# Rotating the first loads over both buffer pools and keeping the last macro tile whole, in a 90-degree rotation of an 8192 x 8192 matrix

## The chip, the cores and the metric

The kernel runs on one core of one Trainium2 chip. The metric is the device time of one execution in microseconds. Times of two kernels are compared within one session on one chip, in interleaved rounds. A ratio is the mean time of one kernel's fast runs over the mean time of the other's fast runs of the same rounds, so it is not quite the ratio of the medians quoted beside it.

The profile names the engines PE (TensorE), DVE (VectorE), ACT (ScalarE) and SP (SyncE, which issues the loads here). PSUM is where PE leaves its results. A "bubble" or "hole" is a stretch in which transfers nearly stop. The "fill" is the work between the landing of the last load and the issue of the last tile's first store. The "drain" is the very end, when most DMA engines have finished.

"Loss" in this document is a stretch of time not used by the DMA: length x (1 - rate / 428 GB/s), where 428 GB/s is the rate of the long middle of the kernel. All 537.55 MB at that rate take 1256 us, so span = 1256 + sum of losses. The rates shown are rounded, so a loss over the long middle can't be read from its rate; it is taken as what is left of the span. The DMA share of a stage can come out slightly over 1.

## The reference

```python
def setup_inputs():
    return {"x": np.random.randn(8192, 8192).astype(np.float32), "k": 1}

def reference(x, k):
    return np.rot90(x, k)
```

Every output element is one input element moved. 268 MB are read and 268 MB are written.

## The kernel before

A macro tile is 1024 rows by 4096 columns, 16 tiles in all. Its rows come in eight loads of 128 rows (2 MB each). DVE reverses the columns of each load into 64 small tiles `ar` (pool of 68); PE transposes them into PSUM; ACT copies PSUM to an output buffer `ot` and issues its store (2 MB). One output needs a chunk from each of the eight loads, so no output of a tile can start before its eighth load has landed.

```python
R = 1024; RT = R // P; W = 4096; CH = 512; G = 4; PW = 2   # P = 128

def macro_tiles(N, M):
    for r0 in range(0, N, R):
        widths = [W] * (M // W)
        if r0 == 0:
            widths[:1] = [4096]
        if r0 + R == N:
            widths[-1:] = [2048, 1024, 1024]      # the last tile in three parts
        ...
# --- cut ---
    a_pool = ctx.enter_context(tc.tile_pool(name="a_pool", bufs=2))
    r_pool = ctx.enter_context(tc.tile_pool(name="r_pool", bufs=68))
    o_pool = ctx.enter_context(tc.tile_pool(name="o_pool", bufs=2))
    # PSUM pool: 2 buffers of [P, PW, R] f32
# --- cut: for each macro tile ---
        for t0 in range(0, RT, q):                # a load brings q = W // C row blocks
            if loads < 2:
                a = o_pool.tile([P, W], dt, tag="o")
            else:
                a = a_pool.tile([P, W], dt, tag="a")
            loads += 1
            nc.sync.dma_start(out=a, in_=x[...])
            # DVE: eight reversing copies a -> ar
        for g0 in range(0, C // P, G):
            ot = o_pool.tile([P, W], dt, tag="o")
            S = PW if last and g0 + G == C // P else G
            for h in range(0, G, PW):
                # PE: for w in range(PW): for t in range(RT): transpose
                nc.scalar.copy(o[:, G - PW - h : G - h, :], ps[:])
                done = h + PW
                if done % S == 0:
                    nc.scalar.dma_start(out=dst, in_=o[...])
```

## Time and profile before

| | before |
|---|---|
| median, before the prediction | 1275.13 us (1272.76 to 1278.19, 3 runs) |
| span of the profiled run | 1274.2 us |
| busy: PE, ACT, DVE | 56%, 37%, 28% |
| DMA share of the span, 100 to 1130 us | 1.01, at 428 GB/s |

From the page of the kernel before: the DMA rate in 40 equal slices of 31.9 us each, and the chain that ended last, by engine.

```profile
GB/s 375 366 427 427 427 428 431 429 428 428 430 428 430 428 427 429 429 429 429 427 427 427 429 427 428 427 427 429 428 427 426 424 423 429 427 425 422 420 408 338
...
DMA 84%; DVE 12%; issue 2%; ACT 1%; PE 0%; DVEq 0%; SPq 0%; ACTq 0%
```

The middle is flat at 428: the DMA is the bound, and only the first two slices and the last few are below it. The table of stages of the kernel before shows the same (the columns are the stretch, its length, busy time and instructions of each engine, the granted PE clock, the DMA share, and GB/s):

```profile
20.00:60.00 40.00, 14.01 (x84) 11.74 (x85) 17.29 (x50) 7.37 (x4) 0.00 (x0) 1.00 0.94 364
...
100.00:1130.00 1030.00, 603.11 (x3360) 578.19 (x3360) 291.37 (x840) 381.39 (x210) 0.00 (x0) 0.74 1.01 428
1130.00:1200.00 70.00, 42.08 (x278) 40.01 (x279) 16.65 (x48) 32.73 (x18) 0.00 (x0) 0.83 1.01 424
1200.00:1248.00 48.00, 26.23 (x172) 24.72 (x170) 9.52 (x28) 19.85 (x11) 0.00 (x0) 0.79 1.00 406
1248.00:1272.00 24.00, 12.85 (x96) 12.06 (x96) 1.58 (x5) 12.87 (x8) 0.00 (x0) 0.79 0.85 354
1272.00:1274.20 2.20, 0.00 (x0) 0.00 (x0) 0.00 (x0) 0.00 (x0) 0.00 (x0) 0.50 0.06 22
```

The stretch 20 to 60 us loses 6.0 us, and all from 1130 us on loses 9.4 us. The Trainium skill ("DMA: Bandwidth & Descriptors", Specifications) gives 435 GB/s as the ceiling of the fabric; the 428 of this trace's middle is within 2% of that, so by that figure the middle has under 2% to give, and the change doesn't touch it.

In the timeline of DVE (start, length, instruction, idle time before it and what ended it) each row of eight copies follows the landing of a load:

```profile
22.76 2.77 DVE L111 COPY ar<-a 128x512 f32<-128x512 f32 x8 [2.12 <-DMA a<-in_x_dram]
29.79 2.77 DVE L111 COPY ar<-a 128x512 f32<-128x512 f32 x8 [4.25 <-DMA a<-in_x_dram]
35.39 2.77 DVE L111 COPY ar<-a 128x512 f32<-128x512 f32 x8 [2.83 <-DMA a<-in_x_dram]
42.46 2.77 DVE L111 COPY ar<-a 128x512 f32<-128x512 f32 x8 [4.29 <-DMA a<-in_x_dram]
47.89 2.77 DVE L111 COPY ar<-a 128x512 f32<-128x512 f32 x8 [2.66 <-DMA a<-in_x_dram]
```

The first of these rows is load 4 of the first tile and the last row is load 8. They are 7.0, 5.6, 7.1 and 5.4 us apart, where a 2.097 MB load takes 4.9 us at 429 GB/s. Only two load buffers turn over there.

In the last 20 us, the timeline of ACT of the kernel before shows copies 5.5 us apart, with waits for stores:

```profile
1251.91 3.63 ACT L133 COPY ot<-ps 128x2048 f32<-128x2048 f32 x2 [1.95 <-PE ps L128]
1255.58 0.55 ACTq L141 DMA_DIRECT2D out_dram<-ot  x1
1257.39 3.64 ACT L133 COPY ot<-ps 128x2048 f32<-128x2048 f32 x2 [1.85 <-DMA out_dram<-ot]
```

### The profile page before, as it was taken

To read this page: it belongs to the slowest core of one execution; us is meant where nothing else is said; L and a number is where in the kernel's file an instruction comes from. 1 tells how busy PE (TensorE), PEld (TensorE's weight loads), DVE (VectorE), ACT (ScalarE), POOL (GpSimd) and SP (SyncE) were. 2 spreads that over 40 slices of the span, in tenths; PEclk is the share of its full clock that TensorE was granted. 3 is DMA by queue.
4 is the path that set the end of the run, shared out by engine and by line. 5 is a ranking of instruction groups with operands and counts; after the bars stand their busy time and mean duration, and the time that the engine had idled before them with its cause. 6 is when DMAs were issued, how large, how long until landed. Compare 5 with 4: busy or idle time off the path is not lost.

```text
span 1274.2 us, 10388 instructions
## 1 busy us (share of the span) xinstructions
PE 719.2 (56%) x4096; PEld 685.5 (54%) x4096; DVE 355.2 (28%) x1024; ACT 466.9 (37%) x257; POOL 0.7 (0%) x6
## 2 busy tenths in 40 slices
PE   1455556556655665556546565565565665665564
PEld 0355556555554655556546555565555554665564
DVE  4422232223222322232223222322232222321210
ACT  0233343334334333343334333433343333434444
POOL 0000000000000000000000000000000000000000
PEclk9968686877777677776886867768777778678878
DMA  9999999999999999999999999999999999999998
GB/s 375 366 427 427 427 428 431 429 428 428 430 428 430 428 427 429 429 429 429 427 427 427 429 427 428 427 427 429 428 427 426 424 423 429 427 425 422 420 408 338
DMA packets 39105, 537.55 MB, mean 422 GB/s; under 512 B 4112, under 2 KB 4112, under 8 KB 6160
## 3 DMA queue, kind: packets, MB, share of 16 engines
q1 hardware_dynamic: 20480, 268.44, 49.8%
q10 hardware_dynamic: 18576, 268.44, 49.8%
q8 instruction: 32, 0.52, 0.2%
q14 instruction: 17, 0.14, 0.0%
HBM read 268.44 MB, written 268.44 MB: 421 GB/s over the span
## 4 chain that ended last, share of the span: by engine, by line
DMA 84%; DVE 12%; issue 2%; ACT 1%; PE 0%; DVEq 0%; SPq 0%; ACTq 0%
DMA a<-in_x_dram 81%; DVE ar L111 12%; DMA out_dram<-ot 3%; ACT ot L133 1%; PE ps L128 0%; DVEq L111 0%; SPq L100 0%; ACTq L133 0%; ACTq L141 0%
## 5 line engine op out<-in xcount | busy, mean ns | idle before, releaser
L128 PE MATMUL ps<-ident,ar 128*128 128x128 f32 x4096 | 719.2, 358 | 543.8 <-ACT ot L133 500.2
L128 PEld LDWEIGHTS ps<-ident,ar 128*128 128x128 f32 x4096 | 685.5, 192 | 577.3 <-ACT ot L133 530.5
L133 ACT COPY ot<-ps 128x2048 f32<-128x2048 f32 x256 | 465.6, 1870 | 789.3 <-DMA out_dram<-ot 733.5
L111 DVE COPY ar<-a 128x512 f32<-128x512 f32 x1024 | 355.2, 421 | 894.4 <-DMA a<-in_x_dram 894.4
L133 ACT ACT_TABLE_LOAD x1 | 1.3, 1283 | 10.9 <-DVE ar L111 10.9
masks.py:199 POOL TENSOR_SCALAR_AFFINE_SELECT ident<-ident 128x128 f32<-128x128 f32 x1 | 0.3, 292 | 0.1
masks.py:197 POOL MEMSET ident<- 128x128 f32 x1 | 0.2, 204 | 0.3 <-POOLq L160 0.3
L160 POOL MEMSET const-bfloat16-1.0<- 128x1 bf16 x1 | 0.1, 102 | 0.0
L160 POOL MEMSET const-uint8-127<- 128x1 uint8 x1 | 0.1, 102 | 0.0
L160 POOL MEMSET const-float32-0.0<- 128x1 f32 x1 | 0.1, 99 | 0.2 <-issue 0.2
L160 POOL MEMSET const-float32-1.0<- 128x1 f32 x1 | 0.1, 99 | 0.0
## 6 DMA issues: line engine op xcount, KB each, us to landing
a<-in_x_dram SPq DMA_DIRECT2D x128, 2048.0 KB, 16.6
out_dram<-ot ACTq DMA_DIRECT2D x127, 2048.0 KB, 15.9
out_dram<-ot ACTq DMA_DIRECT2D x2, 1024.0 KB, 5.7
```

The source lines that it names most:

```text
L111: nc.vector.tensor_copy(out=ar[:], in_=a[:, u, j * CH : (j + 1) * CH].rearrange("r (b m) -> r b m", m=P)[:, :, ::-1],)
L128: nc.tensor.transpose(ps[:, PW - 1 - w, t * P : (t + 1) * P], chunks[t, g * P // CH][:, g % (CH // P), :], ident,)
L133: nc.scalar.copy(o[:, G - PW - h : G - h, :], ps[:])
L160: nc = _bacc.Bacc("TRN2", target_bir_lowering=False, num_devices=1)
```

## The change

At the start, only two of the first eight loads used the output buffers; now loads 3, 4, 7 and 8 do, so all four buffers turn over. At the end, the last macro tile is no longer cut into 2048, 1024 and 1024 columns, and its eight outputs use load and output buffers in turn, since no load needs the load buffers any more.

```diff
+LAST = [4096]
@@ macro_tiles
-        if r0 == 0:
-            widths[:1] = [4096]
         if r0 + R == N:
-            widths[-1:] = [2048, 1024, 1024]
+            widths[-1:] = LAST
@@ loads
-            if loads < 2:
+            if loads < RT and loads % 4 >= 2:
                 a = o_pool.tile([P, W], dt, tag="o")
@@ outputs
-            ot = o_pool.tile([P, W], dt, tag="o")
+            if last and g0 // G % 2 == 0:
+                ot = a_pool.tile([P, W], dt, tag="a")
+            else:
+                ot = o_pool.tile([P, W], dt, tag="o")
```

## The prediction

> **What bounds the kernel.** The DMA engines. In the stretch from 100 to 1130 us the table by stages shows a DMA share of 1.01 and 428 GB/s, and the chain of waits is 84% DMA. PE is busy 56%, ACT 37%, DVE 28%. The Trainium skill ("DMA: Bandwidth & Descriptors", Specifications) gives 435 GB/s as the fabric ceiling; this trace's middle agrees, within 2%. All 537.55 MB at 428 GB/s would take 1256 us of a 1274.2 us span. So about 18 us can be won at all, a part of it unavoidable (first packet, last completion), and only the two ends of the kernel matter.
>
> **Start, before.** The first four loads land 4.9 us apart (DVE starts at 8.1, 13.0, 17.9, 22.8: 2.097 MB each, 429 GB/s). Then only two load buffers turn over: the next four land 7.0, 5.6, 7.1 and 5.4 us apart, and the table by stages shows 351 to 375 GB/s from 20 to 45 us and 282 from 45 to 50. The change has loads 4 to 7 wait for loads 0 to 3, so about three stay in flight. I expect all eight 4.9 us apart: DVE on the eighth at 42.4 us instead of 47.9, first store issued near 48.9 instead of 54.4. That is 5.5 us; the 282 to 416 GB/s dip around 45 to 60 us should shrink too, for 0 to 1.5 us more. Estimate: 6 us, all on the critical path, since everything after is DMA-bound.
>
> **End, before.** Rate by stages: 424 (1130 to 1200), 406 (1200 to 1248), 354 (1248 to 1272), then 2.2 us of almost nothing. Against 428 that loses 0.7 + 2.5 + 4.2 us, plus the final 2 us. The last outputs start copying 5.5 us apart (1251.9, 1257.4, 1263.5), because two output buffers leave ACT waiting for stores; between 1248 and 1250 only 66 GB/s moved.
>
> **End, after.** After the last load lands, all eight outputs of the last tile (16.8 MB) remain, a pure store phase. Per output PE needs 3.7 us at full clock, ACT 3.64 + 0.55 us to issue; a store needs 4.9 to 5.0 us (the store-only stretch 1264 to 1272 averages about 422 GB/s). With four buffers the stores should queue and DMA, not ACT, set the pace. Costs: store-only rate +0.6 us; a possible bubble before the tile's first store, which is ready about 6.5 us after the last load lands, while the previous tile's last two stores cover an estimated 7.7 us: 0 to 2 us. Final latency stays, 2 us. Net gain: 7.4 - 0.6 - 1 = about 6 us. Work totals do not change.
>
> **Prediction.** 1275.1 - 12 = 1263 us, 0.9% faster; 8 in 10 between 1259 and 1270. Faster by over 2%: 0.02; within 2%: 0.97; slower by over 2%: 0.01.
>
> **What would show it.** Start: equal 4.9 us steps of the eight first loads, 425 GB/s or more from 5 to 45 us, DVE on load 8 near 42.4. Middle: unchanged 428 GB/s. End: no rate below 400 between 1130 and the last store except a short bubble; about 40 us without loads; stores landing about 5 us apart; ACT's waits for stores there, yet with DMA busy.
>
> **What would make it wrong.** PE at a lower granted clock in the dense tail (12 matmuls in 2 us at 0.57, so over 5 us per output), making the tail PE-bound: up to +8 us at the end. A store-only rate well under 420 GB/s over 40 us. A larger bubble where loads end. A read-only rate under 429 with continued loading. In the other direction, a gain of up to 15 us if all the losses vanish.

## More of the kernel before

Near 1131 us, in the steady state, a load lands 1.3 us after ACT has begun an output's copies:

```profile
1130.69 3.63 ACT L133 COPY ot<-ps 128x2048 f32<-128x2048 f32 x2 [6.25 <-DMA out_dram<-ot]
1131.95 2.78 DVE L111 COPY ar<-a 128x512 f32<-128x512 f32 x8 [7.11 <-DMA a<-in_x_dram]
```

This distance (from the start of an output's copies to DVE's start on the next landed load) is called the **offset** below.

## The result and the profile after

| | before | after |
|---|---|---|
| median, first session | 1274.65 us (1272.76 to 1278.19, 4 runs) | 1271.05 us (1270.76 to 1271.21, 4 runs) |
| ratio, first session | | 0.9968 (0.9946 to 0.9990) |
| ratio, two later sessions of 5 rounds | | 0.9952 (0.9940 to 0.9965) and 0.9950 (0.9936 to 0.9965) |

The change saves 4 us by the first session and 6 us by the two later ones. The prediction was 12 us. The measured 1271.05 lies 1 us above its range.

From the page of the kernel after, the same two lines:

```profile
GB/s 400 415 431 429 429 428 429 430 428 429 428 429 428 430 430 428 429 429 430 428 428 420 429 429 429 429 429 427 428 422 427 426 421 430 427 427 427 428 342 382
...
DMA 78%; ACT 18%; DVE 1%; PE 1%; issue 1%; ACTq 0%; DVEq 0%
```

The first slices have risen from 375 and 366 to 400 and 415. At the end the losses have moved into the last two slices: one slice has fallen to 342. Stages of the kernel after:

```profile
20.00:60.00 40.00, 14.48 (x90) 11.83 (x90) 20.10 (x59) 8.66 (x5) 0.00 (x0) 0.98 1.01 420
...
1200.00:1210.00 10.00, 5.84 (x32) 5.60 (x32) 2.96 (x10) 3.63 (x2) 0.00 (x0) 0.66 1.00 426
1210.00:1230.00 20.00, 11.62 (x85) 10.87 (x86) 3.81 (x12) 11.01 (x6) 0.00 (x0) 0.83 0.70 295
1230.00:1260.00 30.00, 20.13 (x174) 18.52 (x172) 0.00 (x0) 21.82 (x12) 0.00 (x0) 0.94 1.02 425
1260.00:1266.00 6.00, 0.00 (x0) 0.00 (x0) 0.00 (x0) 0.00 (x0) 0.00 (x0) 0.50 0.95 399
1266.00:1269.20 3.20, 0.00 (x0) 0.00 (x0) 0.00 (x0) 0.00 (x0) 0.00 (x0) 0.50 0.06 26
```

The start works: 20 to 60 us has gone from 364 to 420 GB/s. The store phase works as well: from 1230 to 1260 us there is nothing but stores, at 425 GB/s. Between them, 1210 to 1230 us runs at 295 GB/s, and that is new. The losses of the two traces, computed as said above (the middle as the rest of the spans, 1274.2 and 1269.2 us):

| stretch | before, us lost | after, us lost |
|---|---|---|
| 0 to 20 us | 2.2 | 2.2 |
| 20 to 100 us | 6.4 | 0.7 |
| 100 to 1130 us (rest) | 0.2 | 0.5 |
| 1130 to 1210 us | 1.3 | 0.0 |
| 1210 us to the end | 8.1 | 9.8 (6.2 from 1210 to 1230, 0.2 to 1260, 3.4 to the end) |
| sum | 18.2 | 13.2 |

The start won 5.7 us. The end, from 1130 us on, lost 9.4 us before and 9.8 us after: it won nothing.

DVE of the kernel after, from load 4 on:

```profile
22.80 2.77 DVE L111 COPY ar<-a 128x512 f32<-128x512 f32 x8 [2.12 <-DMA a<-in_x_dram]
27.69 2.78 DVE L111 COPY ar<-a 128x512 f32<-128x512 f32 x8 [2.12 <-DMA a<-in_x_dram]
32.58 2.77 DVE L111 COPY ar<-a 128x512 f32<-128x512 f32 x8 [2.11 <-DMA a<-in_x_dram]
38.26 2.77 DVE L111 COPY ar<-a 128x512 f32<-128x512 f32 x8 [2.90 <-DMA a<-in_x_dram]
43.11 2.77 DVE L111 COPY ar<-a 128x512 f32<-128x512 f32 x8 [2.08 <-DMA a<-in_x_dram]
```

The steps are 4.9 us, but for one of 5.7, and load 8 lands 4.8 us earlier than before (43.1 against 47.9).

The place where the end went wrong, in the timeline of DVE, PE and ACT of the kernel after:

```profile
1211.95 3.63 ACT L137 COPY ot<-ps 128x2048 f32<-128x2048 f32 x2 [6.19 <-DMA out_dram<-ot]
...
1215.62 0.55 ACTq L145 DMA_DIRECT2D out_dram<-ot  x1
1218.09 2.77 DVE L111 COPY ar<-a 128x512 f32<-128x512 f32 x8 [7.05 <-DMA a<-in_x_dram]
...
1218.57 6.39 PE L132 MATMUL ps<-ident,ar 128*128 128x128 f32 x41 [3.72 <-DVE ar L111]
1220.79 1.87 ACT L137 COPY ot<-ps 128x2048 f32<-128x2048 f32 x1 [5.20 <-PE ps L132]
1223.25 1.87 ACT L137 COPY ot<-ps 128x2048 f32<-128x2048 f32 x1 [0.60 <-PE ps L132]
1225.15 0.55 ACTq L145 DMA_DIRECT2D out_dram<-ot  x1
```

At 1215.62 ACT issues the last store of the tile before. At 1218.09 the kernel's last load has landed. Only then can PE finish the first half of the last tile's first output; ACT copies it, waits for PE, copies the second half, and issues the first store of the tile at 1225.15, 7.1 us after the landing. The offset is 6.1 us here (1218.09 - 1211.95), not 1.3. What the DMA does meanwhile, in finer stretches of the kernel after:

```profile
1213.00:1218.00 5.00, 0.98 (x7) 0.74 (x7) 0.00 (x0) 2.59 (x2) 0.00 (x0) 0.73 0.64 267
1218.00:1222.00 4.00, 3.43 (x16) 3.43 (x17) 2.77 (x8) 1.21 (x1) 0.00 (x0) 0.50 0.95 401
1222.00:1224.00 2.00, 2.00 (x20) 2.00 (x19) 0.00 (x0) 1.40 (x2) 0.00 (x0) 0.98 0.08 33
1224.00:1226.00 2.00, 1.79 (x17) 1.55 (x16) 0.00 (x0) 1.33 (x2) 0.00 (x0) 1.00 0.00 0
1266.00:1268.00 2.00, 0.00 (x0) 0.00 (x0) 0.00 (x0) 0.00 (x0) 0.00 (x0) 0.50 0.10 41
```

There are two holes: one before the last load has landed (267 GB/s, with no further load queued behind it), and one after the last old store has gone out (33 and 0 GB/s). From 1210 to 1218 us, before the landing, 1.8 us are lost (331 GB/s), and from 1218 to 1230 us 4.4 us (270 GB/s). The share of 0.08 in 1222 to 1224 and 0.10 in 1266 to 1268 is that of one to two of 16 engines: most engines had run dry while one or two still moved data. The fill also ran on a slow PE, at a granted clock of 0.50 until 1222 us. The Trainium skill ("TensorE: Matmul & The Clock Gate", Part 1) says that the clock is at half until about 3.4 us of sustained activity; this trace agrees (PE resumed at 1218.6, and the clock is 0.98 from 1222 on).

### The profile page after: what moved, and what is told of

Read it like the earlier page. It is cut to its first block, busy times and chain, and to the rows that moved or that the text cites. A ratio compares the mean times of both kernels' runs of the same rounds, so it can differ in the third digit from the quotient of the medians.

```text
span 1269.2 us, 10385 instructions
## 1 busy us (share of the span) xinstructions
PE 708.7 (56%) x4096; PEld 668.1 (53%) x4096; DVE 355.2 (28%) x1024; ACT 467.2 (37%) x257; POOL 0.7 (0%) x6
## 4 chain that ended last, share of the span: by engine, by line
DMA 78%; ACT 18%; DVE 1%; PE 1%; issue 1%; ACTq 0%; DVEq 0%
DMA out_dram<-ot 72%; ACT ot L137 18%; DMA a<-in_x_dram 6%; DVE ar L111 1%; PE ps L132 1%; ACTq L145 0%; ACTq L137 0%; DVEq L111 0%
## 5 line engine op out<-in xcount | busy, mean ns | idle before, releaser
L132 PE MATMUL ps<-ident,ar 128*128 128x128 f32 x4096 | 708.7, 353 | 544.3 <-ACT ot L137 461.5
L132 PEld LDWEIGHTS ps<-ident,ar 128*128 128x128 f32 x4096 | 668.1, 188 | 584.6 <-ACT ot L137 492.4
```

The costliest lines, as they stand in the source:

```text
L132: nc.tensor.transpose(ps[:, PW - 1 - w, t * P : (t + 1) * P], chunks[t, g * P // CH][:, g % (CH // P), :], ident,)
```

## The experiments

Theory A: the start is worth 6 us by itself, and the end is worth nothing because of the fill at the last tile, whatever the start. Theory B: both parts are worth their 6 us alone, but the new start moves the loads against the stores (offset 1.3 to 6.1 us), and that opens the bubble. A third possibility was that the gain of the start is given back in the middle; the table of losses speaks against it (0.2 and 0.5 us). Twelve runs were made, all with correct results. Here they are in one table; the ratio is to the kernel before of the same session.

| kernel | median us | ratio (95% interval) |
|---|---|---|
| session 1: start only | 1269.96 | 0.9953 (0.9941 to 0.9966) |
| end only | 1275.16 | 0.9994 (0.9980 to 1.0008) |
| after, outputs in two buffers | 1273.14 | 0.9976 (0.9963 to 0.9988) |
| after, last load in 4 pieces | 1267.88 | 0.9932 (0.9918 to 0.9945) |
| session 2: after | 1270.39 | 0.9952 (0.9940 to 0.9965) |
| after, shorter fill | 1269.96 | 0.9943 (0.9930 to 0.9957) |
| after, 4 pieces and shorter fill | 1268.00 | 0.9933 (0.9920 to 0.9945) |
| end only, one look | 1273.72 | (single run) |
| session 3: after | 1271.09 | 0.9950 (0.9936 to 0.9965) |
| start only | 1271.70 | 0.9959 (0.9946 to 0.9971) |
| after, last load in 4 pieces | 1268.14 | 0.9928 (0.9916 to 0.9941) |
| after, 2 pieces and shorter fill | 1267.64 | 0.9924 (0.9911 to 0.9938) |

The kernel before had medians of 1276.32, 1276.51 and 1277.19 us in these sessions.

### The start alone

```diff
-LAST = [4096]
+LAST = [2048, 1024, 1024]
-            if last and g0 // G % 2 == 0:
+            if False:
```

> The first tile's loads rotate over both pools as in the kernel after; the last tile is split 2048, 1024, 1024 and all outputs use the output buffers, as before. Theory A (the start is worth 6 us by itself, the end of the change is worth nothing, because a bubble of 6 us opens where the loads end): about 1269 us, no slower than the kernel after (1271). Theory B (start and end each worth about 6 us alone, but the new start shifts the loads against the stores and that spoils the end): also about 1269 us, so this run fixes the size of the start alone. Theory C (the start's gain is given back somewhere in the middle): 1273 us or more.

Once more, beside the kernel after on one chip:

> Start-only once more, beside the kernel after on one chip. If the new end is worth nothing on the new start, within 1 us of the kernel after; if it is worth what the prediction said, 6 us slower than the kernel after.

> The kernel after, on one chip with the start-only kernel, to settle what the new end is worth on the new start: about 1270.5 us, ratio to before 0.995 to 0.997.

The start alone has ratios of 0.9953 and 0.9959, which is 6.0 and 5.2 us. Its stretch from 20 to 60 us lost 0.65 us, as in the kernel after. In session 3 the kernel after was 0.9950 and the start alone 0.9959: the new end is worth 1 us (0.0009 x 1277), with overlapping intervals. So the start's 6 us were predicted well, and nearly the whole of the change's gain is the start. The 1273 us or more that a loss in the middle would have given (theory C) came in neither session.

### The end alone

```diff
-            if loads < RT and loads % 4 >= 2:
+            if loads < 2:
```

> Old start (two loads in output buffers, six in the load buffers), new end (whole last tile, load and output buffers in turn). Theory A (the end is worth nothing whatever the start): 1275 us, as before, with a rate under 200 GB/s for some 5 us after the last load lands. Theory B (the end alone is worth 5 us, because with the old start the last load lands about 1.3 us after the last copy of the tile before began, not 6.1 us, so more store traffic is left to cover the fill): 1269 to 1271 us, bubble of 1 to 2 us.

> The end-only kernel once more (old start, new end), for a second trace. Its five times ran from 1273.5 to 1278.9 us and the trace was of the fastest, with the last load landing 3.1 us after the copy and 2.4 us lost in the bubble. Theory B (the offset of loads against stores sets the bubble): a slower run shows a larger offset and a larger bubble at the end. Theory A (the offset does not matter): a slower run has lost its time elsewhere, at the start or in the middle, with the same bubble.

By time theory A was right: 0.9994, under 1 us. The second run was to be a slower one, but at 1273.72 us it was as fast as the first traced run (1273.47), so it could not show where a slow run loses its time. It does show a larger offset with a larger bubble, as theory B has it. In the two traces of the end alone (first two rows from the first, the others from the second):

```profile
1218.39 3.63 ACT L137 COPY ot<-ps 128x2048 f32<-128x2048 f32 x2 [6.18 <-DMA out_dram<-ot]
1221.45 2.77 DVE L111 COPY ar<-a 128x512 f32<-128x512 f32 x8 [7.00 <-DMA a<-in_x_dram]
```

```profile
1217.03 3.63 ACT L137 COPY ot<-ps 128x2048 f32<-128x2048 f32 x2 [6.64 <-DMA out_dram<-ot]
...
1215.00:1230.00 15.00, 10.62 (x68) 9.50 (x66) 2.77 (x8) 8.79 (x5) 0.00 (x0) 0.77 0.73 310
```

In the second trace DVE began on the last load at 1220.72. Offsets and losses around the last landing (from 1210 to 1230 us both traces of the end alone give the same losses as in the shorter stretches of the table):

| trace | offset, us | lost around the last landing, us |
|---|---|---|
| end alone, first trace | 3.1 | 2.4 (1220 to 1230) |
| end alone, second trace | 3.7 | 4.1 (1215 to 1230: 15 x (1 - 310/428)) |
| after, third trace | 4.8 | 5.8 (1210 to 1230) |
| after, first and second trace, and after with two buffers | 6.1 to 6.2 | 6.2 to 7.2 (1210 to 1230) |

So among these traces a smaller offset goes with a smaller bubble. The offset is not fixed by the code, though. Near 1131 us, where the 1.3 was read, the two traces of the end alone have 3.5 and 4.2 us, although up to there they run the same code as the kernel before. The eleven traces with the new start have 4.9 us (the four of session 3) or 6.1 to 6.2 us (the other seven) at that place. So the new start went with a larger offset in every trace, but only three traces have the old one, and its offsets differ by 3 us among themselves. Still the end alone did not become 5 us faster, as theory B expected. In its first trace the end, from 1130 us on, lost 6.5 us instead of 9.4 (in its second 8.0), and the old start, with the same code, happened to lose 0.8 us more than in the trace of before. That trace was of its fastest run (1273.47); the others went up to 1278.87. The spread of kernels with the old start is 3 to 5 us and that of kernels with the new start 0.3 to 3 us. What makes up that spread was not found, and how much of the end's gain in a single trace survives in the mean stays open within 1 to 3 us. The interaction that theory B claims is not seen in the times: start alone 6.0, end alone 0.8, both 6.1 and 6.4 us. The 1.3 us of offset between the kernel after in sessions 2 and 3 did not show in its ratio either (0.9952 and 0.9950).

### The outputs of the last tile in two buffers

```diff
-            if last and g0 // G % 2 == 0:
+            if False:
```

> The kernel after, but the last tile's outputs use the two output buffers alone. If the four buffers in turn are what keeps the store phase at the rate of the DMA, the last eight outputs come 5.5 us apart as in the end before instead of 4.9: 4 to 6 us slower than the kernel after, 1275 to 1277. If they do nothing (the store phase has two stores in flight either way), 1271.

The ratio is 0.9976, against 0.9950 and 0.9952 of the kernel after in other sessions, so about 3 us are lost; the expectation was 4 to 6. The ACT timeline of this run shows waits for stores that the kernel after has not, and its stage 1230 to 1260 us runs at 379 GB/s against 425:

```profile
1230.00:1260.00 30.00, 20.31 (x176) 18.82 (x174) 0.00 (x0) 18.18 (x10) 0.00 (x0) 1.00 0.90 379
...
1238.94 3.63 ACT L137 COPY ot<-ps 128x2048 f32<-128x2048 f32 x2 [2.41 <-DMA out_dram<-ot]
1243.84 3.63 ACT L137 COPY ot<-ps 128x2048 f32<-128x2048 f32 x2 [1.26 <-DMA out_dram<-ot]
1249.38 3.64 ACT L137 COPY ot<-ps 128x2048 f32<-128x2048 f32 x2 [1.91 <-DMA out_dram<-ot]
```

Four buffers keep the stores at the rate of the DMA, as the prediction said. From 379 to 425 GB/s over 30 us is 3.2 us.

### The last load in four pieces

```diff
+            pieces = 4 if last and t0 + q == RT else 1
+            for p in range(pieces):
+                c1, c2 = p * C // pieces, (p + 1) * C // pieces
                 nc.sync.dma_start(
-                    out=a, in_=x[..., c0 : c0 + C]...)
+                    out=a[:, :, c1:c2], in_=x[..., c0 + c1 : c0 + c2]...)
```

> The kernel after, but the very last load (row block 7 of the last tile) is issued as four loads of 1024 columns, so the first output's columns are there about 4 us or more before the last columns land. Theory A and B alike (the bubble is the 7 us from the last load's landing to the first store's issue, minus what stores are left in flight): 3 to 5 us faster than the kernel after, 1266 to 1268, and the stretch at under 200 GB/s is gone. If the bubble has another cause (stores slow to start, the granted clock), no change: 1271.

> The last load in four pieces once more, now beside the kernel after on one chip: 2 to 3 us faster than the kernel after, about 1268 us.

The ratios are 0.9932 and 0.9928; in session 3 that is 2.8 us faster than the kernel after (0.0022 x 1277), as the second text expected and a little under the 3 to 5 us of the first. The first store of the last tile was issued at 1222.00 instead of 1225.15. So most of the bubble is a matter of the fill, and not of stores that start slowly. A smaller hole was left; here are the stages of this run and, in the next part, the same of the run that closes it:

```profile
1221.00:1223.00 2.00, 2.00 (x20) 1.85 (x19) 0.00 (x0) 1.33 (x2) 0.00 (x0) 1.00 0.12 49
1263.00:1264.50 1.50, 0.00 (x0) 0.00 (x0) 0.00 (x0) 0.00 (x0) 0.00 (x0) 0.50 0.16 66
```

### A shorter fill, alone and with the pieces

```diff
-                for w in range(PW):
-                    for t in range(RT):
+                order = [(w, t) for w in range(PW) for t in range(RT)]
+                if last and g0 == 0:      # row block by row block
+                    order = [(w, t) for t in range(RT) for w in range(PW)]
+                for w, t in order:
...
-            S = PW if last and g0 + G == C // P else G
+            S = PW if last and g0 in (0, C // P - G) else G
```

> The kernel after, unchanged, so that the next two runs have it on the same chip: 1271 us, ratio to before 0.996 to 0.997, the last load landing about 6.1 us after the last copy of the tile before began, and some 6 us of transfer lost between 1210 and 1230 us, as in its first trace.

> The kernel after with a shorter fill and no other load: for the first output of the last tile the transposes of both column groups of a half go row block by row block, so that two and not nine remain when the last load lands, and the output is stored in two halves, so the first store needs one copy, not two. Theory (the bubble is the time from the last load's landing to the first store's issue, less the store traffic left): first store issued about 3 us after the last load's first copy instead of 7.1, bubble 4 us shorter, 1267 us. Rival (the store phase starts slowly for a reason of the DMA itself): 1270 to 1271.

The kernel after came out as before, with a ratio of 0.9952 where 0.996 to 0.997 was expected. The shorter fill alone gave 1.1 us (0.9943 against 0.9952, overlapping intervals), not 4. Its ACT timeline says why:

```profile
1219.45 1.87 ACT L139 COPY ot<-ps 128x2048 f32<-128x2048 f32 x1 [3.71 <-PE ps L134]
1222.87 1.87 ACT L139 COPY ot<-ps 128x2048 f32<-128x2048 f32 x1 [1.54 <-PE ps L134]
1222.92 2.38 ACTq L147 DMA_DIRECT2D out_dram<-ot  x2
```

The first half was copied by 1221.32, but in the trace both issues stand behind the second copy in ACT's order of instructions (in the source the first issue comes before it), and that copy waited for PE. The first store left at 1222.92, 4.7 us after the landing and not 3. From 1210 to 1230 us the trace loses 5.2 us, and that of the kernel after from the same session 7.2 us.

> Both at once: the last load in four pieces and the shorter fill. In the run with four pieces alone 2.4 us of transfer were still lost from 1220 to 1225 us, with the first store issued at 1222.0; its first half had been copied by 1218.6. Theory: 2 us faster than the four pieces alone, about 1266 us, ratio to before 0.991 to 0.992, and hardly a bubble. Rival: the two remedies treat the same time and do not add: 1267 to 1268.

Stages of this run, with the pieces and the shorter fill together:

```profile
1221.00:1223.00 2.00, 1.43 (x14) 1.19 (x12) 0.00 (x0) 2.00 (x2) 0.00 (x0) 1.00 1.02 428
1261.00:1264.50 3.50, 0.00 (x0) 0.00 (x0) 0.00 (x0) 0.00 (x0) 0.00 (x0) 0.50 0.14 59
```

The hole at 1221 to 1223 us has gone from 49 to 428 GB/s: there is no bubble. The time did not fall: 1268.00, ratio 0.9933 against 0.9932 and 0.9928. The rival was right that the two do not add, and the trace shows where the time went: the drain at the very end is longer. The last 3.5 us of transfers use a DMA share of 0.14, about two of 16 engines, where the four pieces alone had such a tail for some 1.5 us in the trace shown and the kernel before hardly any (in half-microsecond stretches its share is 1.09 up to 1272.0, then 0.21 and 0.04). The second trace of the four pieces fits: its hole was smaller (216 GB/s from 1220.5 to 1222 us), its tail was as long as here (a share of 0.16 from 1261.0 to 1264.5 us), and its run took 1267.54 us against 1267.72 here, in another session. While most engines stood idle in the hole of the four pieces, a share of 0.12, two engines, was still at work. Filling the hole for the other 14 let them finish earlier and did nothing for those two. That they are the same two engines in the hole and at the end, and so that they set the time, is argued and not shown, since the profile does not number them.

The Trainium skill ("DMA: Bandwidth & Descriptors", Why a DMA increments its semaphore by 16 and not by 1) says that up to 16 engines finish independently and that only the full count means landed. These traces agree with the first part: a share of 0.08 to 0.16 for 1.5 to 3.5 us is one to three engines finishing after the rest.

### Two pieces and the shorter fill

The diff is the two above, with two pieces in place of four.

> The last load in two pieces of 2048 columns and the shorter fill. The four pieces of 1024 columns moved at 369 to 373 GB/s in 1200 to 1210 us, a loss of 1.3 us, so larger pieces should lose less. If the time is set by the mean rate of the 16 DMA engines: 0.5 to 1 us faster than with four pieces, about 1267. If it is set by the one or two engines that in earlier traces still moved data while the others had run dry (DMA share 0.1 at 1221 to 1223 us with four pieces, 0.12 in the last 2 us of the kernel after): no faster than with four pieces, about 1268.

It measured 1267.64 us, ratio 0.9924: 0.5 us faster than four pieces in the same session, with overlapping intervals, between the two expectations. The test is weaker than planned, since the two pieces did not lose less on the whole: 427 GB/s from 1200 to 1210 us against 373 of the four pieces with the shorter fill, but 384 against 429 from 1210 to 1230, together 0.8 us more. That it was no slower all the same speaks for the engines that finish last, and against the mean rate, as what sets the time. Its end again has 3.5 us at a share of 0.11 (1261.0 to 1264.5). This is the fastest kernel, 9.7 us faster than the kernel before and 3.3 us faster than the kernel after (0.0026 x 1277). Four pieces are not told apart from it.

## Why the prediction was wrong

- **"What bounds the kernel": right.** The middle stayed at 428 GB/s, and only the ends moved.
- **Start, 6 us: right.** The trace shows 5.7 us less lost from 20 to 100 us, and the start alone measured 6.0 and 5.2 us. The eighth load's copies began at 43.1 us (predicted 42.4, before 47.9), the first store was issued at 49.6 (predicted 48.9, before 54.4).
- **Store phase: right.** 425 GB/s with nothing but stores (predicted 422); four buffers give about 3 us over two. The feared slow PE clock did not appear in the store phase: PE took 3.74 us for each output there. The waits of ACT for stores that the prediction expected there did not come: ACT waited 0.67 us for PE before each output and had issued its last store at 1255.3.
- **"A possible bubble before the tile's first store ... 0 to 2 us": wrong; this step failed.** It measured 6.2 us of lost transfer, 4.4 of it from the landing on. The step that was mis-sized is the cover: "the previous tile's last two stores cover an estimated 7.7 us". By the expectation of the end alone it goes with an offset of 1.3 us, read from the trace of before; the prediction does not write the working out. In the first trace of the kernel after the offset was 6.1 us: the last load lands 2.5 us after the last old store was issued, not 2.4 us before. The old stores were through by about 1222 us, 4 us and not 7.7 after the landing, and the first new store was issued 7.1 us after it (predicted 6.5). The prediction took the relation between two streams from one trace of the old kernel, and in no other trace was it found again (3.5 and 4.2 us with the old start, 4.9 to 6.2 with the new). A second hole, 267 GB/s from 1213 to 1218 us, was not in the sum at all: no load was queued behind the last one, which was issued at 1201.26, and the last old store was issued only at 1215.62. That this left the DMA short even before the landing is read from this order and was not tested.
- **"Final latency stays, 2 us": mis-sized.** From 1260 us on the kernel after lost 3.4 us, as one or two engines finished after the others; the last 2.2 us of before lost 2.1.
- **Sum.** Predicted for the end: 7.4 - 0.6 - 1 = 6 us. Measured: 1 us by the times of session 3, and -0.4 us by the two traces. With the 5 to 6 us of the start that is about the 4 to 6 us seen.
- **Open.** In the trace a smaller offset goes with a smaller bubble, but the end alone with a smaller offset gained under 1 us in its mean time. So the other offset goes with the mis-sized cover, but it is not shown that the new start alone made it so, nor that the end would have paid its 6 us with the old offset. That the fill costs time is shown by the four pieces (2.8 us); that the last engines take back the rest is argued from the runs without a bubble.

## What to carry to other kernels

Where a DMA-bound kernel ends, count how much store traffic is left when the last load lands and set it against the time from that landing to the first new store; read that relation from a trace of the kernel that will run, since here it differed from kernel to kernel, and by 3 us between executions of the same code. Issuing the last load in pieces, in the order in which outputs need them, was worth 2 to 3 us here; a further cut of the bubble was worth nothing, as far as the traces tell because a few DMA engines were already behind the rest. To judge what a gap in the transfers costs, look not only at the mean rate but at whether some engines still work in it.

## What the Trainium skill lacked or had wrong

- "DMA: Bandwidth & Descriptors", Latency and other measured facts: it tells of two DMA engines that are usually slower (7 and 15) and puts them down, as a best guess, to the software descriptor path. Here both data queues are of the kind hardware_dynamic, and still one to three of 16 engines finished 1.5 to 3.5 us after the rest (DMA share 0.08 to 0.16). Whether they are those two can't be told, since the profile does not number them. A possible cause that no run tested: two 16 KB packets of the instruction queue in the last 44 us of the kernel after.
- The same page has nothing on how far apart the engines end with more stores in flight: with two output buffers the share fell from 1.09 to 0.21 and 0.04 within 1 us at the end (before), with four it was 0.10 from 1266 to 1268 us (after), and with four and no bubble 0.14 for 3.5 us. The kernel after with two buffers, the direct comparison, ended as sharply as the kernel before: 0.60, 0.08 and 0.00 in half-microsecond stretches from 1269.0 us.
- The same page, Where 436 GB/s comes from, says in one sentence that the HBM side (about 358 GB/s) binds transfers between HBM and SBUF. That sentence does not hold for one core alone, as the page's own single-core measurement of 425 GB/s says too: here one core moved 428 GB/s with loads and stores together, and 425 with stores alone.
- No page tells of the offset between a load stream and a store stream, nor that it differs between executions of the same code: near 1131 us it was 1.3, 3.5 and 4.2 us in three traces with the old start, and 4.9 to 6.2 us in eleven with the new.
